# Small columns grouped and padded, so that every wide tile starts on a 512-byte line of its partition

## The chip, the cores and the metric

The kernel runs on one core of one Trainium2 chip. The metric is device time in microseconds (us), the median of three runs; the profile is one execution, taken by the hardware profiler. A core has a matrix engine (PE, whose weight loads are listed as PEld), and DVE, ACT and POOL for elementwise work; SP issues transfers. All tiles here live in the on-chip memory of 128 partitions, and PE writes its results into eight banks of its own (the tiles `pa`, `pb`, `pc`, `pt`).

## What is computed

A two-layer transformer over 512 tokens of 1024 features, in float32. Around each mixer stand two half-weighted gated feed-forward blocks of 2816 hidden features; the first mixer joins sparse and dilated attention, the second is a latent attention.

```python
def _swiglu(x, w_gate, w_up, w_down):
    return (jax.nn.silu(x @ w_gate) * (x @ w_up)) @ w_down
...
def _rms_norm(x, g):
    xf = x.astype(jnp.float32)
    y = xf * lax.rsqrt(jnp.mean(xf * xf, axis=-1, keepdims=True) + NORM_EPS)
    return (y * g.astype(jnp.float32)).astype(x.dtype)
```

The stages run one after another: feed-forward f0, the even mixer (sparse and dilated), f1, f2, the latent mixer, f3, a last norm.

## The kernel before

Features lie on partitions and the 512 tokens along them, so an activation tile is 128 x 512 float32, 2048 bytes of each partition. To keep float32 accuracy every operand is split into a high and a low part, and `mm3` (L142 to L146) makes one product out of three matmuls: weights high with activations high (L144), weights high with activations low (L145), weights low with activations high (L146). Each matmul loads a 128 x 128 block of weights and streams 512 columns of activations past it.

A feed-forward block has two kinds of stretch. Gate and up: for each of 22 hidden tiles, 8 `mm3` into `pa` (gate) and 8 into `pb` (up), with the normalised input `xh`, `xl` as the stream. Down: for each of 8 outputs and each half of the hidden tiles, 11 `mm3` into `pc` or `pt`, with the activations `fah`, `fal` as the stream. The weights come in both cases as chunks of 128 x 1024 (`w`, loaded by SP), split by ACT into `wh` (L128) and by DVE into `wl` (L129); two chunks are held ahead. In the mixers, projections stream `xh`, `xl` too; the even mixer's output projection streams `oh`, `ol`; the latent one's queries and keys stream `cnh`, `cnl`; values are made with the activations as weights and 256 columns of `wh` as the stream.

Where a tile lies on its partition follows from the order in which tiles are first asked for. The pool `keep` lasts for the whole program; `ff`, `ev` and `ml` lie behind it, one after another in the same space. A tile takes its bytes, rounded up to 32. The program starts with 16,512 bytes of other use, 128 bytes past a 512-byte line. So the wide tiles are shifted against the lines by the small ones ahead of them: `x` and `ident` start 128 bytes behind a line; `ones`, `mhalf` and `g` (32 + 32 + 256 bytes) push `xh`, `xl`, `of` and `t` to 448; three `rcol` and two `rv` (160 bytes) push the row factors, `w`, `wh`, `wl` and all that follows to 96; in the even mixer, `pos`, `gt`, `mn` and others push once or twice more. The blocks of 128 columns that one matmul takes of a chunk are 512 bytes wide, so all of them share the chunk's offset.

| tiles (start within a 512-byte line) | before | after |
|---|---|---|
| `xh`, `xl` (stream of gate, up and most projections) | 448 | 0 |
| `w`, `wh`, `wl` (weights of nearly all matmuls) | 96 | 0 |
| `fah`, `fal` (stream of down) | 96 | 0 |
| `oh`, `ol` (stream of the even output projection) | 224 | 0 |
| `cnh`, `cnl` (stream of latent queries and keys) | 96 | 0 |
| `q`, `kh`, `kl`, `v`, `p` of the even mixer | 224 | 0 |
| `ident`, `x` | 128 | 0 |

Of the kernel before, what the change touches and what calls it, by code (L numbers as in the profile page):

```python
# [3 lines left out]
P = 128  # L4
D, SEQ, FF = 1024, 512, 2816
# [8 lines left out]
# column ranges of the even mixer's input projection  # L14
# [3 lines left out]
# blocks of a transposed probability tile: 0 zeros, 1-4 keys 0-127 (queries 0..3), 5-7 keys  # L18
# 128-255 (queries 1..3), 8 keys 384-511 (query 3), 9-10 keys 256-383 (queries 2, 3)
# [10 lines left out]
# The mixers' plans: heads' softmax jobs, and after each the other work. q, k: projections of a pair of  # L30
# heads' queries and keys; v: values; s, c: compression; p: compressed probabilities; o: a chunk of the
# output projection; in the latent mixer l: low-rank inputs, u, w: weights, r: rotary keys.
# [21 lines left out]
def keys(u):  # L54
    """The chunks of weights that a piece of work reads."""
    mla, c, n = u.isupper(), u[0].lower(), u[1:]
    if c == "v" and n in "aA":
        return [("ev_vsw", i) for i in range(3)]
    n = int(n)
    if mla:  # L60
        return {"L": [("mla_in", n)], "W": [("mla_uq", n)], "Y": [("mla_ukv", n)],
                "O": [("mla_out", n)]}.get(u[0], [])
    return {"q": [("ev_in", n)], "k": [("ev_in", n)], "s": [("ev_in", 4 + n)], "o": [("ev_out", n)],
            "c": [("cmp_w1", n, 0), ("cmp_w1", n, 1)], "v": [("ev_vb", n, 0), ("ev_vb", n, 1)]}.get(c, [])


def strided(t, b):
    """Columns 16 n + 2 l + b of t as [partitions, l, n], n < 31."""
    return bass.AP(tensor=t.tensor, offset=t.offset + b, ap=[t.ap[0], [2, 16], [16, 31]])


class Core:
    def __init__(self, tc, ctx, aps):
        self.tc, self.nc, self.a, self.used = tc, tc.nc, aps, -1
        self.keep = ctx.enter_context(tc.tile_pool(name="keep", bufs=1))
        self.ps = ctx.enter_context(tc.tile_pool(name="ps", bufs=2, space=PSUM))
        nc = self.nc
        self.x = [self.keep.tile([P, SEQ], F32, name=f"x{k}") for k in range(KT)]
        self.ident = self.keep.tile([P, P], F32, name="ident")
        self.ones = self.keep.tile([P, 1], F32, name="ones")  # L80
        self.mhalf = self.keep.tile([P, 4], F32, name="mhalf")
        self.g = self.keep.tile([P, 60], F32, name="g")
        nc.vector.memset(self.ones, 1.0)
        nc.vector.memset(self.mhalf, -0.5)
# [15 lines left out]
    def plan(self, stages):  # L100
        """The order in which chunks of weights are used."""
        todo = []
        for st in stages:
            if st in FFNS:
                name, l, _ = FFNS[st]
                for h in range(2):
                    for f in range(h * HF, h * HF + HF):
                        todo += [(name + "_g", l, f), (name + "_u", l, f)]
                    todo += [(name + "_d", l, h, c) for c in range(HF)]
            elif st != "n":  # L110
                for u in flat(EVEN if st == "e" else MLA):
                    todo += keys(u)
        self.todo, self.ready, self.ahead = todo, [], 2

    def fetch(self):
        """Emits the load of the next chunk and, but for compression weights, its split."""
        nc, kp = self.nc, self.keep
        key = self.todo[len(self.ready)]
        src = self.a[key[0]][key[1:]]
        cols = src.shape[1]  # L120
        w = kp.tile([P, 1024], F32, name="w", bufs=3)
        nc.sync.dma_start(w[:, :cols], src)
        if key[0] == "cmp_w1":
            self.ready.append((key, w))
            return
        h = kp.tile([P, 1024], F32R, name="wh", bufs=3)
        l = kp.tile([P, 1024], F32R, name="wl", bufs=3)
        nc.scalar.activation(h[:, :cols], w[:, :cols], AF.Copy)  # L128
        nc.vector.tensor_tensor(l[:, :cols], w[:, :cols], raw(h[:, :cols]), OP.subtract)  # L129
        self.ready.append((key, (h, l)))  # L130

    def chunk(self, *key):
        """A chunk of weights, [128, columns], as its high and low parts; the next ones are under way."""
# [3 lines left out]
        got, tiles = self.ready[i]  # L137
# [10 lines left out]
    def split(self, src, g, tags, bufs):  # L148
        """src [128, 512] times the column g, as high and low parts."""
# [7 lines left out]
    def squares(self, tiles):  # L157
        """Tiles whose features' sum is that of the squares of `tiles`."""
# [10 lines left out]
    def rstd(self, parts, n, before=None):  # L169
        """1/rms over n features from their squares: a column for each block of tokens. With `before`,  # L170
        columns, it is that of the features times `before`, and has this factor in it."""
# [6 lines left out]
        col = kp.tile([P, 4], F32, name="rcol", bufs=3)  # L178
        v = kp.tile([P, 4], F32, name="rv", bufs=2)
# [11 lines left out]
    def spread(self, col, row):  # L191
        """The row `row` of the columns `col`, on all partitions."""
# [58 lines left out]
    def job(self, sb, scores, mask, PT, o, v, start, stop, gate=None, after=None, factor=None):  # L251
        """One head of one branch in three steps: the normalised probabilities [128, (qt, keys)],
        their transposes as high and low parts, and o [(high, low) of V's features, queries] += V . P."""
# [3 lines left out]
        def soft():  # L257
            pt = st["p"] = sb.tile([P, 1280], F32, name="p", bufs=2)
            for qt in range(4):
# [4 lines left out]
                mn = sb.tile([P, 4], F32, name="mn", bufs=8)  # L264
# [34 lines left out]
    @staticmethod  # L299
    def pipe(groups, jobs, do):  # L300
        """Runs a plan, [(names of jobs, other work after each)]: the softmax of a job goes before the
        rest of the job ahead of it."""
# [33 lines left out]
    def values(self, sb, parts, xs, scale=None, more=None):  # L336
        """V of four heads with tokens on partitions: [128, kt, head, (high, low)]. Columns after
        the 256 of V go to `more`."""
# [3 lines left out]
        m = SEQ // c                     # blocks of tokens in a bank  # L342
# [25 lines left out]
    def out_proj(self, oh, parts, name, c):  # L368
        """Chunk c of the output projection, (outputs, pairs of heads, 128): x += its product."""
# [17 lines left out]
    def even(self, gi):  # L387
        nc, a, kp = self.nc, self.a, self.keep
        with self.tc.tile_pool(name="ev", bufs=1, reuse_waits="tile") as sb:
# [16 lines left out]
            nc.gpsimd.tensor_tensor(SR, SR, R, OP.mult)  # L406
            PT = self.pt_tiles(sb)
            q, kd, V, O, C, oh = {}, {}, {}, {}, {}, {}
# [13 lines left out]
            def qstack(i):  # L422
                """Two heads' queries times -1/8, each with its high and low parts stacked."""
# [7 lines left out]
            def kdup(i):  # L431
                """Two heads' keys: high parts twice, low parts twice."""
# [23 lines left out]
            def finish(pair, j):  # L456
                """Fold a head's two parts; after the second head, split the pair."""
# [32 lines left out]
            def stack(i):  # L490
                """Keys or values to compress plus their positions: rows (l mod 2, feature), columns
                (l // 2, group, block)."""
# [14 lines left out]
            def compress(i):  # L507
# [16 lines left out]
                if i == 0:  # L524
                    nc.tensor.matmul(vp[:, :64], w2[:, 0, :], z, start=True, stop=True)
                    kcmp = C["k"] = sb.tile([P, 64], F32, name="kcmp")
                    nc.vector.tensor_copy(kcmp, vp[:, :64])
# [13 lines left out]
            C["g"] = sb.tile([P, 4, 24], F32, name="gt")  # L541

            def gate(kt, p):
                """The sigmoids of a block of tokens' gates."""
# [11 lines left out]
            def cmp_probs(g):  # L556
                """The compressed branch's probabilities for four heads: keys (head, n) on partitions."""
# [7 lines left out]
                st = sb.tile([P, 3, 16], F32, name="st", bufs=2)  # L565
# [38 lines left out]
    def mla(self, gi):  # L604
        nc, a, kp = self.nc, self.a, self.keep
        with self.tc.tile_pool(name="ml", bufs=1, reuse_waits="tile") as sb:
            xs, rc, R = self.norm(gi)
            # even heads have (content, rotary, rotary with its halves swapped) on partitions,
            # odd heads (rotary, swapped, content)
# [18 lines left out]
            def low(i):  # L628
                """The low-rank inputs: queries' but for their tokens' factors (0, 1), keys' and
                values' (2), the keys' rotary part (3)."""  # L630
# [17 lines left out]
            def factors(i):  # L648
                """The tokens' factors: of keys and values (2) or queries (1)."""
# [7 lines left out]
            def rotary(n):  # L657
                """The rotary part of two heads' keys."""
# [94 lines left out]
def constants(np):  # L753
    """Tables that depend on the shapes alone."""
# [3 lines left out]
    d = p + 384 - j                      # query minus key, for the last block of queries  # L758
# [27 lines left out]
def layout(np, i):  # L786
    """The inputs as the chip reads them: each chunk of weights contiguous on its partitions."""
# [14 lines left out]
    def feat(w):  # L802
        """[K, 128 n] -> n chunks [128, (k, 128)]."""
# [3 lines left out]
    def out_parts(w, parts):  # L807
        """[(pair, 128), 1024] -> for each part of the pairs, chunks [128, (outputs, pair, 128)]."""
# [8 lines left out]
    def tok(w, n):  # L817
        """[1024, c] -> chunks [128, (n k, c)]."""
        w = w.reshape(KT, P, -1)
        pad = -KT % n  # L820
        if pad:
# [10 lines left out]
    d["pos"] = np.concatenate([w, w])   # [(group, feature), k or v, l mod 2, l // 2]  # L832
# [8 lines left out]
                 axis=3)                # [k, 128, pair, parity, 128]  # L841
# [24 lines left out]
```

## Time and profile before

| what | value |
|---|---|
| median of 3 runs | 1989.07 us (1989.05 to 1989.41) |
| span of the profiled execution | 1983.8 us |
| time outside the span, against the median | 5.3 us |
| PE busy | 1945.0 us, 98% |
| PEld, DVE, ACT, POOL busy | 81%, 53%, 38%, 21% |
| granted clock of PE, mean | 0.995 |

The page gives the profiled execution by its span, from the first to the last instruction; the time around it is taken from the median. Since PE is busy for 98% of it, the length of one matmul and their number nearly make the time. A matmul's listed duration overlaps with that of the next, so the pace is read from the distance of starts.

### The profile page before, as it was taken

To read this page: it belongs to the slowest core of one execution; us is meant where nothing else is said; L and a number is where in the kernel's file an instruction comes from. 1 tells how busy PE (TensorE), PEld (TensorE's weight loads), DVE (VectorE), ACT (ScalarE), POOL (GpSimd) and SP (SyncE) were. 2 spreads that over 40 slices of the span, in tenths; PEclk is the share of its full clock that TensorE was granted. 3 is DMA by queue.
4 is the path that set the end of the run, shared out by engine and by line. 5 is a ranking of instruction groups with operands and counts; after the bars stand their busy time and mean duration, and the time that the engine had idled before them with its cause. 6 is when DMAs were issued, how large, how long until landed. Compare 5 with 4: busy or idle time off the path is not lost.

```text
span 1983.8 us, 23309 instructions
## 1 busy us (share of the span) xinstructions
PE 1945.0 (98%) x9086; PEld 1601.1 (81%) x9086; DVE 1058.2 (53%) x1594; ACT 754.9 (38%) x1230; POOL 408.2 (21%) x390
## 2 busy tenths in 40 slices
PE   8999999999998999999999999999999999999997
PEld 6888888878887788888888888888878878888885
DVE  5443444467888744344444543554399764434442
ACT  4321223347586532222232222223388543212231
POOL 4110111164445311001110100111156331101111
PEclk9999999999999999999999999999999999999998
DMA  4322222322111132222322232222310223222221
GB/s 161 96 96 95 96 96 96 112 90 96 54 44 33 46 105 95 95 96 96 96 96 95 86 97 99 91 96 96 121 44 22 64 85 96 95 96 96 96 96 54
DMA packets 49422, 174.37 MB, mean 88 GB/s; under 512 B 5792, under 2 KB 6176, under 8 KB 49312
## 3 DMA queue, kind: packets, MB, share of 16 engines
q1 hardware_dynamic: 47808, 169.64, 26.3%
q0 software_dynamic: 640, 2.10, 0.3%
q8 instruction: 71, 1.16, 0.2%
q10 hardware_dynamic: 864, 1.15, 0.2%
q14 instruction: 39, 0.32, 0.1%
HBM read 170.76 MB, written 2.10 MB: 87 GB/s over the span
## 4 chain that ended last, share of the span: by engine, by line
PE 92%; DVE 4%; ACT 2%; POOL 1%; issue 1%; DMA 0%; DVEq 0%; POOLq 0%; ACTq 0%
PE pa L146 11%; PE pa L145 11%; PE pa L144 11%; PE pb L146 9%; PE pb L145 9%; PE pb L144 9%; PE pc L144 4%; PE pc L145 4%; PE pc L146 4%; PE pt L146 4%; PE pt L144 4%; PE pt L145 4%; PE pc L293 2%; PE pt L282 2%; PE pb L452 1%
## 5 line engine op out<-in xcount | busy, mean ns | idle before, releaser
L128 ACT ACTIVATE wh<-w 128x1024 fp32r<-128x1024 f32 (+1 forms) x313 | 331.3, 1059 | 894.5 <-issue 347.3
L129 DVE TENSOR_TENSOR wl<-w,wh 128x1024 fp32r<-128x1024 f32 (+1 forms) x313 | 482.1, 1541 | 234.9 <-ACT wh L128 234.7
L144 PE MATMUL pa<-xh,wh 128*128 128x512 f32 x928 | 368.2, 397 | 8.6 <-ACT xh L153 8.1
L146 PE MATMUL pa<-xh,wl 128*128 128x512 f32 x928 | 369.1, 398 | 0.0
L145 PE MATMUL pa<-xl,wh 128*128 128x512 f32 x928 | 367.7, 396 | 0.3 <-DVE xl L154 0.3
L232 POOL TENSOR_TENSOR fa<-fs,fu 128x512 f32<-128x512 f32 x88 | 117.9, 1339 | 1070.3 <-DVE fu L228 636.9
L146 PE MATMUL pb<-xh,wl 128*128 128x512 f32 x704 | 280.0, 398 | 0.0
L145 PE MATMUL pb<-xl,wh 128*128 128x512 f32 x704 | 278.5, 396 | 0.1
L144 PE MATMUL pb<-xh,wh 128*128 128x512 f32 x704 | 277.5, 394 | 0.0
L144 PEld LDWEIGHTS pa<-xh,wh 128*128 128x128 f32 x928 | 174.9, 188 | 50.0 <-ACT xh L153 8.1
L228 DVE TENSOR_TENSOR fu<-pb,rrow 128x512 f32<-128x512 f32 x88 | 60.8, 691 | 280.8 <-PE pb L146 280.8
L145 PEld LDWEIGHTS pa<-xl,wh 128*128 128x128 f32 x928 | 174.8, 188 | 43.4 <-DVE xl L154 1.6
L146 PEld LDWEIGHTS pa<-xh,wl 128*128 128x128 f32 x928 | 174.8, 188 | 40.5 <-DVE wl L129 0.2
L145 PEld LDWEIGHTS pb<-xl,wh 128*128 128x128 f32 x704 | 132.3, 188 | 35.8 <-DVE xl L154 2.5
L144 PEld LDWEIGHTS pb<-xh,wh 128*128 128x128 f32 x704 | 132.4, 188 | 32.2 <-ACT xh L153 0.4
L146 PEld LDWEIGHTS pb<-xh,wl 128*128 128x128 f32 x704 | 132.2, 188 | 30.8 <-DVE wl L129 0.2
L226 DVE TENSOR_TENSOR fg<-pa,rrow 128x512 f32<-128x512 f32 x88 | 60.8, 691 | 147.5 <-PE pa L146 147.4
L145 PE MATMUL pc<-fal,wh 128*128 128x512 f32 x352 | 137.1, 389 | 0.0
L144 PE MATMUL pc<-fah,wh 128*128 128x512 f32 x352 | 137.0, 389 | 0.0
L146 PE MATMUL pc<-fah,wl 128*128 128x512 f32 x352 | 136.9, 389 | 0.0
L146 PE MATMUL pt<-fah,wl 128*128 128x512 f32 x352 | 136.9, 389 | 0.0
L144 PE MATMUL pt<-fah,wh 128*128 128x512 f32 x352 | 136.9, 389 | 0.0
(184 smaller groups left out, 2737.4 us busy)
## 6 DMA issues: line engine op xcount, KB each, us to landing
w<-f_g SPq DMA_DIRECT2D x88, 512.0 KB, 3.4
w<-f_u SPq DMA_DIRECT2D x88, 512.0 KB, 3.4
w<-f_d SPq DMA_DIRECT2D x88, 512.0 KB, 3.4
w<-ev_in SPq DMA_DIRECT2D x16, 512.0 KB, 3.4
w<-ev_out SPq DMA_DIRECT2D x8, 512.0 KB, 3.6
w<-mla_out SPq DMA_DIRECT2D x8, 512.0 KB, 3.6
x<-x POOLq DMA_DIRECT2D x8, 256.0 KB, 7.0
w<-ev_vb SPq DMA_DIRECT2D x4, 512.0 KB, 3.6
```

Of the source, the lines that this page charges most:

```text
L128: nc.scalar.activation(h[:, :cols], w[:, :cols], AF.Copy)
L129: nc.vector.tensor_tensor(l[:, :cols], w[:, :cols], raw(h[:, :cols]), OP.subtract)
L144: nc.tensor.matmul(out, wh, xh, start=start, stop=False)
L145: nc.tensor.matmul(out, wh, xl, start=False, stop=False)
L146: nc.tensor.matmul(out, wl, xh, start=False, stop=stop)
L226: nc.vector.tensor_tensor(t, pgu[0], R, OP.mult)
L228: nc.vector.tensor_tensor(u, pgu[1], R, OP.mult)
L232: nc.gpsimd.tensor_tensor(a, s, u, OP.mult)
L282: nc.tensor.transpose(ps[:, i * P:(i + 1) * P], pt[:, c:c + P], self.ident)
L293: nc.tensor.matmul(ps[:, q0:], v(kt), PT[j][:, b, :], start=start and kt == 0 and j == 0, stop=stop and kt == 3 and j == 1)
L452: nc.tensor.matmul(ps[:, :n], q[qi][:, qt * P:(qt + 1) * P], kd[ki][j][:, :n], start=j == 0, stop=j == 1)
```

## The change

No operation is added, dropped or moved: on each engine the instructions stand in the same order, with the same shapes, and the transfers too. Three small columns and `rv` are asked for ahead of everything, `rcol` gets 16 buffers instead of 3 (16 x 32 = 512 bytes), the small tiles of the even mixer are asked for together ahead of the wide ones (the two `st` as tiles of their own instead of two buffers), and `mn` has 16 buffers instead of 8 in the latent mixer. With that each group of small tiles fills whole lines together with what stands around it, and every wide tile starts at 0. As by-products, some reuses of a column buffer are gone, and with them a second semaphore of one POOL, four ACT and ten DVE instructions that wait for another one anyway. Comments and document strings are dropped as well, so line numbers after differ.

```diff
+        self.small()
         self.x = [self.keep.tile([P, SEQ], F32, name=f"x{k}") for k in range(KT)]
         self.ident = self.keep.tile([P, P], F32, name="ident")
...
+    def small(self):
+
         self.ones = self.keep.tile([P, 1], F32, name="ones")
         self.mhalf = self.keep.tile([P, 4], F32, name="mhalf")
         self.g = self.keep.tile([P, 60], F32, name="g")
...
+        self.rv()
+
+    def rv(self):
+        return self.keep.tile([P, 4], F32, name="rv", bufs=2)
...
-        col = kp.tile([P, 4], F32, name="rcol", bufs=3)
-        v = kp.tile([P, 4], F32, name="rv", bufs=2)
+        col = kp.tile([P, 4], F32, name="rcol", bufs=16)
+        v = self.rv()
...
-                mn = sb.tile([P, 4], F32, name="mn", bufs=8)
+                mn = self.stats(sb)
...
+    def stats(sb):
+
+        return sb.tile([P, 4], F32, name="mn", bufs=8 if sb.name == "ev" else 16)
...
+            q, kd, V, O, C, oh = {}, {}, {}, {}, {}, {}
+            C["g"] = sb.tile([P, 4, 24], F32, name="gt")
+            C["k"] = sb.tile([P, 64], F32, name="kcmp")
+            C["st"] = [sb.tile([P, 3, 16], F32, name=f"st{g}") for g in range(2)]
+            self.stats(sb)
             PT = self.pt_tiles(sb)
-            q, kd, V, O, C, oh = {}, {}, {}, {}, {}, {}
...
-                st = sb.tile([P, 3, 16], F32, name="st", bufs=2)
+                st = C["st"][g]
```

## Rows read from the trace of the kernel before

**Rows 1.** The page: span; busy time of the engines; granted clock of PE by slice.

```profile
span 1983.8 us, 23309 instructions
...
PE 1945.0 (98%) x9086; PEld 1601.1 (81%) x9086; DVE 1058.2 (53%) x1594; ACT 754.9 (38%) x1230; POOL 408.2 (21%) x390
...
PEclk9999999999999999999999999999999999999998
```

**Rows 2.** The chain that ended last, shares of the span by engine.

```profile
PE 92%; DVE 4%; ACT 2%; POOL 1%; issue 1%; DMA 0%; DVEq 0%; POOLq 0%; ACTq 0%
```

**Rows 3.** Windows: stretch, length, busy us of PE, PEld, DVE, ACT, POOL, clock, DMA.

```profile
60.00:130.00 70.00, 70.00 (x301) 56.31 (x300) 35.20 (x32) 20.29 (x25) 8.03 (x7) 1.00 0.29 92
150.00:184.00 34.00, 34.00 (x152) 28.16 (x151) 10.63 (x11) 6.37 (x6) 0.00 (x0) 1.00 0.31 99
720.00:790.00 70.00, 70.00 (x302) 56.31 (x301) 33.44 (x31) 19.66 (x24) 7.75 (x6) 1.00 0.30 98
820.00:854.00 34.00, 34.00 (x152) 28.15 (x151) 10.48 (x11) 6.37 (x6) 0.00 (x0) 1.00 0.29 93
```

**Rows 4.** Timeline of PE in gate and up of f0: start, duration, instruction.

```profile
100.60 0.39 PE L144 MATMUL pb<-xh,wh 128*128 128x512 f32 x1
100.83 0.39 PE L145 MATMUL pb<-xl,wh 128*128 128x512 f32 x1
101.07 0.40 PE L146 MATMUL pb<-xh,wl 128*128 128x512 f32 x1
101.30 0.39 PE L144 MATMUL pb<-xh,wh 128*128 128x512 f32 x1
```

**Rows 5.** Timeline of PE in down of f0, a triple's start and the next one's.

```profile
160.14 0.39 PE L144 MATMUL pt<-fah,wh 128*128 128x512 f32 x1
...
160.82 0.39 PE L144 MATMUL pt<-fah,wh 128*128 128x512 f32 x1
```

**Rows 6.** Groups of instructions by line: count, then busy us and mean ns.

```profile
L144 PE MATMUL pa<-xh,wh 128*128 128x512 f32 x928 | 368.2, 397 | 8.6 <-ACT xh L153 8.1 <-DVE x L384 0.5
...
L144 PE MATMUL pb<-xh,wh 128*128 128x512 f32 x704 | 277.5, 394 | 0.0
...
L144 PE MATMUL pc<-fah,wh 128*128 128x512 f32 x352 | 137.0, 389 | 0.0
...
L144 PE MATMUL pt<-fah,wh 128*128 128x512 f32 x352 | 136.9, 389 | 0.0
...
L144 PE MATMUL pa<-oh,wh 128*128 128x512 f32 x64 | 25.9, 412 | 4.8 <-DVE x L384 4.7
```

**Rows 7.** Timeline of PE, even output projection, five triples apart.

```profile
665.52 0.39 PE L144 MATMUL pa<-oh,wh 128*128 128x512 f32 x1
...
669.01 0.39 PE L144 MATMUL pa<-oh,wh 128*128 128x512 f32 x1
```

**Rows 8.** Timeline of PE, a latent query's six matmuls and what follows.

```profile
1456.93 0.40 PE L144 MATMUL pa<-cnh,wh 128*128 128x512 f32 x1
...
1458.32 0.27 PE L282 MATMUL pt<-ident,p 128*128 128x128 f32 x1
```

**Rows 9.** Timeline of PE, values of the even mixer, four triples apart.

```profile
381.26 0.28 PE L351 MATMUL pa<-wh,xh 128*128 128x256 f32 x1
...
382.67 0.28 PE L351 MATMUL pa<-wh,xh 128*128 128x256 f32 x1
```

**Rows 10.** Timeline of PE, values of the latent mixer, two triples apart.

```profile
1440.71 0.28 PE L351 MATMUL pa<-wh,cnh 128*128 128x256 f32 x1
...
1441.43 0.28 PE L351 MATMUL pa<-wh,cnh 128*128 128x256 f32 x1
```

**Rows 11.** Waits: who waited for whom, us in total, times, longest.

```profile
POOL rcol L186 <- DVE rv L181: 58.4, 7, 12.5
...
ACT p L268 <- DVE mn L265: 29.7, 31, 2.7
...
PE pa L144 <- ACT xh L153: 8.1, 1, 8.1
```

More of the change, by code (lines that the diff above doesn't have):

```diff
@@ L77, in __init__ @@
         nc = self.nc
+        self.small()
         self.x = [self.keep.tile([P, SEQ], F32, name=f"x{k}") for k in range(KT)]
         self.ident = self.keep.tile([P, P], F32, name="ident")
+        nc.vector.memset(self.ones, 1.0)
+        nc.vector.memset(self.mhalf, -0.5)
+    def small(self):
         self.ones = self.keep.tile([P, 1], F32, name="ones")
@@ L82, in __init__ @@
         self.g = self.keep.tile([P, 60], F32, name="g")
-        nc.vector.memset(self.ones, 1.0)
-        nc.vector.memset(self.mhalf, -0.5)
+        self.rv()
+    def rv(self):
+        return self.keep.tile([P, 4], F32, name="rv", bufs=2)
     def load(self):
@@ L297, in job @@
         return soft, trans, pv
+    @staticmethod
+    def stats(sb):
+        return sb.tile([P, 4], F32, name="mn", bufs=8 if sb.name == "ev" else 16)
     @staticmethod
@@ L525, in compress @@
                     nc.tensor.matmul(vp[:, :64], w2[:, 0, :], z, start=True, stop=True)
-                    kcmp = C["k"] = sb.tile([P, 64], F32, name="kcmp")
-                    nc.vector.tensor_copy(kcmp, vp[:, :64])
+                    nc.vector.tensor_copy(C["k"], vp[:, :64])
                     return
@@ L539, in compress @@
                         nc.vector.tensor_tensor(vc[s, j, 64:128], vg[s], raw(vc[s, j, 0:64]), OP.subtract)
-            C["g"] = sb.tile([P, 4, 24], F32, name="gt")
             def gate(kt, p):
```

## Prediction

> **What bounds the kernel now.** First the page: PE is busy for 1945.0 of 1983.8 us, with its clock granted in full nearly throughout, that is at 2.4 GHz [rows 1]. Then the chain of work that ended last: 92% of it is PE [rows 2], and PE's longest wait in the whole program, 8.1 us, is the start-up [rows 11]. So a change reaches the time by the pace of matmuls, or not at all; what DVE, ACT, POOL and the transfers do counts only where PE waits for them, and that is under 39 us (1983.8 - 1945.0), spread over start, end and the mixers.
>
> Next the pace, stage by stage, in the windows [rows 3]. Two stretches of gate and up, 70 us each, hold 300 matmuls (301 and 302 with those cut at the edges): 70.0 / 300 = 233.3 ns each. Two stretches of down, 34 us each, hold 150: 226.7 ns. In both PE is busy throughout and the granted clock is 1.00. The timeline shows the same without an average: one `mm3` takes 0.70 us in gate and up (100.60 to 101.30) [rows 4] and 0.68 us in down (160.14 to 160.82) [rows 5].
>
> This is the row on which all rests. The two kinds of stretch issue the same thing, weight blocks of 128 columns and streams of 512 in the order of L144 to L146, yet one is 3% slower. Four things differ: where the stream lies (448 against 96 bytes behind a line, weights at 96 in both), the result banks, the length of a group (24 against 33 matmuls), and what the other engines do meanwhile. The last can be struck out: DVE is busy for half of gate and up (35.20 of 70) and ACT for under a third (20.29) [rows 3], in pieces, while the triple stays at 0.70 us whether or not they run. What is left is the place of the stream, or the banks and group length.
>
> A third place helps. In the even output projection, with the stream at 224 and weights at 96, five triples take 669.01 - 665.52 = 3.49 us, 232.7 ns a matmul [rows 7], into the bank that gate uses. So three distances between stream and weights give three paces: 0 bytes 226.7, 128 bytes 232.7, 352 bytes 233.3 ns. Equal offsets give the shortest.
>
> **The change, part by part.** (1) Gate and up. After the change stream and weights both start at 0, so their distance is 0 as in down today. Of triples into `pb` there are 704, all from the blocks; into `pa` 928, of which 704 are gate and 224 projections [rows 6]. So 1408 triples go from 0.70 to 0.68 us: 1408 x 0.020 = 28.2 us saved. The stretch must then not meet another bound. Down already runs at 0.68 us a triple with the same chunks to split, at DVE 10.63 and ACT 6.37 of 34 us [rows 3], and gate and up leave half of DVE free; they are 3% shorter afterwards, no more.
>
> (2) The mixers' wide matmuls: 224 triples with `xh`, `xl` and 64 with `oh`, `ol` [rows 6]. There PE hops between short groups. A query of the latent mixer has equal offsets already (96 and 96), and its six matmuls take 1458.32 - 1456.93 = 1.39 us, 231.7 ns each [rows 8], not 226.7. So equal offsets bring 233.3 - 231.7 = 1.6 ns at least and 6.6 ns at most: 672 x 1.6 = 1.1 us to 672 x 6.6 = 4.4 us for the projections, and 192 x (232.7 - 231.7) = 0.2 us to 192 x 6.0 = 1.2 us for the output projection. These groups are nearest to the query's, so I take 2.0 us of the 1.3 to 5.6.
>
> (3) Shorter streams. Values of the even mixer, with unlike offsets, need (382.67 - 381.26) / 12 = 117.5 ns for 256 columns [rows 9]; those of the latent mixer, with equal ones, (1441.43 - 1440.71) / 6 = 120 ns [rows 10]. Equal offsets do not help there and might cost 2.5 ns on 288 matmuls of this kind, 0.7 us; I take 0.3. Transposes and single columns show no unlike pair to compare; I take 0.
>
> (4) Down stays at 0 distance: 0 in the likeliest case; its bounds are in the rivals.
>
> (5) The other engines' operations and the transfers read and write from new places. What hides them is PE: without that cover only the 8.1 us of the start and the few waits in the mixers show it, and a few per cent of these is under 1 us. I take 0.
>
> (6) The dropped second semaphores: POOL's reciprocal roots waited 58.4 us for DVE [rows 11], and the softmax exponentials 29.7 us for DVE, so the other semaphore was never last. 0.
>
> Sum: 28.2 + 2.0 - 0.3 = 29.9 us. The profiled span becomes 1983.8 - 29.9 = 1953.9; with 5.3 us around it (1989.07 - 1983.8) that is 1959.2 us.
>
> A rule of the Trainium skill speaks against this. Its page "TensorE: Matmul & The Clock Gate", section "Step-by-step: what each phase is for", gives PE two independent read ports, so that loading the next weights takes nothing from the running matmul; by that the place of one against the other would not matter and the sum would be 0. The trace does not fit it well: the page's gap of about 216 ns for 512 columns is 226.7 at best here, and the gap does differ between stretches.
>
> **The rivals.** *No change.* The 3% come from the banks or the group length, and offsets do nothing. For it: `pa` and `pb` hold the triples of 0.70 us and `pc` and `pt` those of 0.68, without exception in the long stretches. Against it: the bank `pa` shows 231.7 with equal offsets [rows 8] and 232.7 and 233.3 with unlike ones; that is little, since the first comes from short groups. Time: 1989. The Trainium skill's page "SBUF — State Buffer", section "Specifications (TRN2)", gives on-chip lines of 16 bytes; by that rule, too, nothing would move, as 96, 224 and 448 are all multiples of 16. The rows here show no such line.
>
> *The place behind the line counts, not the distance.* 96, 224 and 448 bytes behind a line give 226.7, 232.7 and 233.3: the pace also falls with the offset itself. Then 0 is better than 96, and down gains as well. A straight line through the first two gives 222.2 ns at 0, one through the outer two 224.9. Gate and up would save 1408 x 3 x 11.1 = 46.9 or x 8.4 = 35.5 us, down 704 x 3 x 4.5 = 9.5 or x 1.8 = 3.8 us, with the 2 us of the mixers 58.4 or 41.3 in all: 1931 to 1948. Against it: three points, and the step from 224 to 448 is small.
>
> *Slower.* A start on a multiple of 64 bytes costs: 448 is one and pays 233.3, 96 is not and pays 226.7. After the change all starts are such multiples; gate and up keep 0.70 us and down goes from 0.68 to 0.70: 704 triples (352 into each of two banks [rows 6]) x 0.020 = 14.1 us, 2003 us. It decides as soon as gate and up gain less than 14.1 us, that is when their triple stays above 0.69. Against it: 224 is no such multiple and pays 232.7.
>
> **How the numbers follow.** Equal distance, as forecast: 0.57, with a range of its own of 1955 to 1961 (the bounds of parts 2 and 3). The place behind the line: 0.14. No change: 0.17. Slower: 0.08. What I have not thought of: 0.04, half of it slower and a quarter each faster and the same. The runs before lie within 0.36 us, and under 0.2%, 4 us, I call it no change. So faster 0.57 + 0.14 + 0.01 = 0.72, the same 0.17 + 0.01 = 0.18, slower 0.08 + 0.02 = 0.10. The range reaches from the upper end of the second case, 1945 (a fifth of it kept), over the forecast to no change, 1990: 0.57 + 0.03 + 0.17 + 0.02 = 0.79. It leaves out most of the second case and the slower one.
>
> **What would show it.** In gate and up, a triple of 0.68 us, 309 matmuls in 70 us; in down 0.68 as before. If gate and up reach 0.68 and down falls below, the place behind the line counts. If both stand as they were, it was banks or groups. If down rises to 0.70, it is the multiple of 64. Groups of the other engines should keep their mean durations where no other engine disturbs them, and PE's waits should stay at some 39 us. I am wrong if the pace depends on the pair in a way that three distances do not show, for instance if 0 and 0 collide where 96 and 96 do not, or if the faster PE runs ahead of the split of a chunk, which would appear as waits of PE for `wh` or `wl`.

## The result: 1957.5 us after 1989.1, and the profile after

The changed kernel takes 1957.49 us (median of four runs, 1954.03 to 1958.47) against 1989.06 (1988.98 to 1989.41) for the kernel before: a ratio of 0.9838 with an interval of 0.9824 to 0.9852. The profiled execution took 1958.47 us with a span of 1956.7.

The page after, to be read beside [rows 1] and [rows 2]:

```profile
span 1956.7 us, 23295 instructions
...
PE 1916.9 (98%) x9086; PEld 1604.4 (82%) x9086; DVE 1057.6 (54%) x1594; ACT 754.9 (39%) x1230; POOL 407.7 (21%) x390
...
PE 93%; DVE 4%; ACT 2%; issue 1%; POOL 0%; DMA 0%; DVEq 0%; ACTq 0%; POOLq 0%
```

As many matmuls as before (9086), and 28.1 us less of PE busy; DVE, ACT and POOL within 0.6 us of where they were. So PE's pace changed, and the busy times of the others did not. The windows of the kernel after say where; columns as in [rows 3], gate and up in the first and third, down in the second and fourth:

```profile
60.00:128.00 68.00, 68.00 (x301) 56.33 (x301) 34.31 (x32) 19.94 (x26) 7.75 (x6) 1.00 0.31 97
150.00:184.00 34.00, 34.00 (x151) 28.16 (x151) 10.64 (x11) 6.99 (x7) 0.00 (x0) 1.00 0.29 93
720.00:788.00 68.00, 68.00 (x302) 56.31 (x301) 34.35 (x32) 19.93 (x26) 7.75 (x6) 1.00 0.31 97
820.00:854.00 34.00, 34.00 (x152) 28.15 (x151) 10.67 (x11) 7.23 (x7) 0.00 (x0) 1.00 0.31 100
```

Gate and up now issue in 68 us the 301 matmuls that took 70 [rows 3]; down issues what it did. The granted clock is 1.00 in both kernels here, so it isn't the clock. Without an average, from the timeline of PE after (start, duration, instruction): 48 triples apart in gate and up, then 32 apart in down.

```profile
61.19 0.39 PE L152 MATMUL pa<-xh,wh 128*128 128x512 f32 x1
...
93.83 0.39 PE L152 MATMUL pa<-xh,wh 128*128 128x512 f32 x1
...
151.63 0.39 PE L152 MATMUL pc<-fah,wh 128*128 128x512 f32 x1
...
173.39 0.39 PE L152 MATMUL pt<-fah,wh 128*128 128x512 f32 x1
```

(93.83 - 61.19) / 48 = 0.680 us a triple, and (173.39 - 151.63) / 32 = 0.680. A matmul is still shown as 0.39 us long, as in [rows 4]: its duration overlaps the next one's, and only the distance between starts shows the pace.

The whole span can be laid out by one kind of instruction, the sums of the norms, which open and close the stages. From the chain of work that ended last (start, us, what; seven of these rows in each kernel), before:

```profile
24.33 1.68 PE pt L176 x16
384.01 1.46 PE pt L176 x14
688.07 1.68 PE pt L176 x16
1051.79 1.46 PE pt L176 x14
1419.25 1.46 PE pt L176 x14
...
1610.22 1.68 PE pt L176 x16
1968.68 1.74 PE pt L176 x14
```

and after:

```profile
24.40 1.68 PE pt L184 x16
377.45 1.46 PE pt L184 x14
682.59 1.68 PE pt L184 x16
1039.43 1.46 PE pt L184 x14
1399.87 1.46 PE pt L184 x14
...
1589.36 1.68 PE pt L184 x16
1941.11 2.36 PE pt L184 x14
```

Differences of neighbouring rows are the stages. The four feed-forward blocks become shorter by 6.63 (359.68 to 353.05), 6.88, 7.02 and 6.71 us, 27.24 together; the latent mixer becomes shorter by 1.48; the even mixer becomes longer by 1.08 (304.06 to 305.14), the end by 0.47 and the start by 0.07. Sum: 27.1 us saved, the difference of the spans.

The even mixer is longer although a quiet stretch of its output projection is quicker (shown with the mixers below). Windows of PE alone in it (length, busy us and matmuls, granted clock, DMA share, GB/s), before:

```profile
425.00:440.00 15.00, 12.03 (x62) 0.89 0.33 102
500.00:512.00 12.00, 9.39 (x54) 1.00 0.17 47
```

and after:

```profile
425.00:440.00 15.00, 12.08 (x58) 0.77 0.40 128
500.00:512.00 12.00, 8.94 (x42) 0.86 0.15 44
```

The two pairs don't hold quite the same work, since the mixer begins 6.6 us earlier after the change. In both stretches PE had waited (12 of 15 and some 9 of 12 us busy). The granted clock was at its lower level, 1.2 GHz, for a part of the first stretch before (0.89), and for a part of both after (0.77 and 0.86). Such stretches also differ between runs of one kernel: the runs after have mean clocks of 0.993 to 0.996 and spans of 1956.7 to 1952.3 us, and later runs of the kernel before go from 1985.88 us at 0.995 to 1990.45 at 0.992. The profiled execution of the kernel before was a short one: time and span lie some 1.8 us apart in every run here that lists both, so a span of 1983.8 stands for some 1985.6 us, 3.5 below the median.

### The profile page after: what moved, and what is told of

Its sections match the earlier page's. It is cut to its first block, busy times and chain, and to the rows that moved or that the text cites. A ratio compares the mean times of both kernels' runs of the same rounds, so it can differ in the third digit from the quotient of the medians.

```text
span 1956.7 us, 23295 instructions
## 1 busy us (share of the span) xinstructions
PE 1916.9 (98%) x9086; PEld 1604.4 (82%) x9086; DVE 1057.6 (54%) x1594; ACT 754.9 (39%) x1230; POOL 407.7 (21%) x390
## 4 chain that ended last, share of the span: by engine, by line
PE 93%; DVE 4%; ACT 2%; issue 1%; POOL 0%; DMA 0%; DVEq 0%; ACTq 0%; POOLq 0%
PE pa L152 11%; PE pa L153 11%; PE pa L154 11%; PE pb L153 9%; PE pb L154 9%; PE pb L152 9%; PE pt L154 4%; PE pc L154 4%; PE pc L152 4%; PE pt L152 4%; PE pc L153 4%; PE pt L153 4%; PE pc L301 2%; PE pt L290 2%; PE pb L469 1%; DVE wl L137 1%
## 5 line engine op out<-in xcount | busy, mean ns | idle before, releaser
L136 ACT ACTIVATE wh<-w 128x1024 fp32r<-128x1024 f32 (+1 forms) x313 | 331.3, 1059 | 867.0 <-issue 352.1
L137 DVE TENSOR_TENSOR wl<-w,wh 128x1024 fp32r<-128x1024 f32 (+1 forms) x313 | 481.8, 1540 | 235.5 <-ACT wh L136 234.9
L153 PE MATMUL pa<-xl,wh 128*128 128x512 f32 x928 | 363.3, 391 | 0.0
L154 PE MATMUL pa<-xh,wl 128*128 128x512 f32 x928 | 362.9, 391 | 0.0
L240 POOL TENSOR_TENSOR fa<-fs,fu 128x512 f32<-128x512 f32 x88 | 117.5, 1335 | 1043.8 <-DVE fu L236 974.3
L154 PE MATMUL pb<-xh,wl 128*128 128x512 f32 x704 | 274.3, 390 | 0.0
L153 PE MATMUL pt<-fal,wh 128*128 128x512 f32 x352 | 136.9, 389 | 0.0
```

The costliest lines, as they stand in the source:

```text
L153: nc.tensor.matmul(out, wh, xl, start=False, stop=False)
L154: nc.tensor.matmul(out, wl, xh, start=False, stop=stop)
L240: nc.gpsimd.tensor_tensor(a, s, u, OP.mult)
```

## The experiments

**Theory and rivals.** The theory is that the pace depends on where the stream lies against the weights. The rivals are the stream's own place behind a line, a start on a line, a start on a multiple of 64 bytes, and the banks or the length of a group.

**1. Equal distance, off the line.** The kernel before with 352 unused bytes, which move weights and the stream of down from 96 to 448, where the stream of gate and up already lies.

```diff
     # in rms, ahead of rrow
+    self.pad = getattr(self, "pad", None) or self.keep.tile([P, 88], F32, name="pad")
```

> The kernel before with one unused tile of 352 bytes ahead of the row factors: weights and down's stream move from 96 to 448, the place where the stream of gate and up already lies; nothing starts on a line. Equal distance (forecast): gate and up 0.68 us a triple, down 0.68, time 1989.1 - 28.2 - about 1 = 1960 us; the even output projection keeps 128 bytes of distance (64 against 448) and stays near 232 ns a matmul. Place of the stream (448 is a bad place whatever the weights do): gate and up stay at 0.70 and down rises to 0.70, 1989.1 + 14.1 = 2003 us. Start on a line needed: not below 1989 us.

1960.96 us (1959.11 to 1961.22), ratio 0.9856 (0.9842 to 0.9871). Windows as above, gate and up, then down:

```profile
60.00:128.00 68.00, 68.00 (x302) 56.31 (x301) 34.34 (x32) 19.93 (x26) 7.75 (x6) 1.00 0.28 99
150.00:184.00 34.00, 34.00 (x152) 28.15 (x151) 10.61 (x11) 7.03 (x7) 0.00 (x0) 1.00 0.26 93
```

The pace is that of the changed kernel with both at 448, a multiple of 64 and not on a line. The stream of gate and up hasn't moved at all. So three rivals fall: its own place, the start on a line, and the multiple of 64.

**2. On the line, but apart.** The changed kernel with 160 unused bytes: the stream of gate and up stays at 0, weights and the stream of down go to 160.

```diff
     # in rms, ahead of rrow
+    self.pad = getattr(self, "pad", None) or self.keep.tile([P, 40], F32, name="pad")
```

> The changed kernel with 160 unused bytes ahead of the row factors: the stream of gate and up stays at 0, weights and down's stream go to 160, so gate and up have again the distance of before (352 = -160 in 512), and down has equal offsets off the line. Equal distance: gate and up 0.70 us, down 0.68, time 1957.5 + 28.2 + about 1 = 1987 us. Start of the stream on a line suffices: gate and up 0.68, time about 1958 us.

1987.81 us (1985.03 to 1989.11, ten runs), ratio 0.9993 (0.9983 to 1.0003), as before.

```profile
60.00:128.00 68.00, 68.00 (x293) 54.72 (x292) 34.04 (x31) 20.19 (x25) 8.02 (x7) 1.00 0.27 93
150.00:184.00 34.00, 34.00 (x152) 28.15 (x151) 10.63 (x11) 6.37 (x6) 0.00 (x0) 1.00 0.29 100
```

Gate and up are back at 293 matmuls in 68 us, 0.70 us a triple; down, whose stream moved along with its weights, is untouched. Banks and groups are those of the changed kernel. Distance alone gives the whole gain back.

**3 and 4. A map of distances.** The feed-forward blocks alone (both mixers left out); the eight tiles of x lie at 0, 64, ..., 448 bytes, so that every group runs through eight places; then the same with weights moved by 192 bytes (the last line of the edit).

```diff
-        h = self.keep.tile([P, SEQ], F32R, name=tags + "h", bufs=bufs)
+        self.nsplit = getattr(self, "nsplit", -1) + 1
+        c = (0, 16, 32, 48, 64, 80, 96, 112)[self.nsplit % 8]
+        h = self.keep.tile([P, SEQ + 128], F32R, name=tags + "h", bufs=bufs)[:, c:c + SEQ]
...
+    self.pad = getattr(self, "pad", None) or self.keep.tile([P, 48], F32, name="pad")
```

> Feed-forward blocks and last norm alone (both mixers left out), weights at 0, and the eight tiles of the normalised input at 0, 64, 128, ... 448 bytes, one place for each k. Equal distance: k = 0 at 226.7 ns a matmul, k = 2 (128 bytes) near 232.7, the others slower than 226.7; the mean of a group of 24 between 226.7 and 233.3. Multiples of 64 alone: all eight alike. Down at 0 and 0: 0.68 us a triple.

> As the map of 64 steps, with the weights at 192 instead of 0 (mixers left out). Equal distance: the same eight paces, moved by three places: k = 3 at 226.7 ns, k = 5 (128 bytes) as k = 2 of the first map. Place of the stream: the same eight paces at the same k as in the first map.

One run each: 1496.48 and 1495.90 us. Timeline of PE in the first kernel, four tiles of one group (0, 64, 128 and 192 bytes) and the next start:

```profile
102.16 0.39 PE L152 MATMUL pa<-xh,wh 128*128 128x512 f32 x1
...
102.85 0.40 PE L152 MATMUL pa<-xh,wh 128*128 128x512 f32 x1
...
103.55 0.40 PE L152 MATMUL pa<-xh,wh 128*128 128x512 f32 x1
...
104.25 0.39 PE L152 MATMUL pa<-xh,wh 128*128 128x512 f32 x1
...
104.94 0.39 PE L152 MATMUL pa<-xh,wh 128*128 128x512 f32 x1
```

0.69, 0.70, 0.70, 0.69: neighbours of unlike places blur each other, and the order of 64, 128 and 192 bytes here isn't that of the single distances below. What can be read off is the period, in the medians over all groups. For 0, 64, ..., 448 bytes they are 690, 698, 697, 695, 690, 698, 697, 695 ns: the row repeats after 256 bytes, not after 512. With weights at 192: 698, 697, 695, 690, 698, 697, 695, 690. The same row moved by three places of 64: it follows the distance, and the distance counts modulo 256.

**5 to 7. One distance for a whole block**, which takes the blur out: the same edit with one place for each of the four blocks (still without mixers).

```diff
-        c = (0, 16, 32, 48, 64, 80, 96, 112)[self.nsplit % 8]
+        c = (4, 8, 16, 32)[self.nsplit // 8]     # then (1, 2, 24, 40), then (48, 56, 60, 64)
```

> Feed-forward blocks and last norm alone (both mixers left out), weights at 0; the stream of gate and up lies at one place for a whole block, 16 bytes behind the weights' place in f0, 32 in f1, 64 in f2, 128 in f3. Step (any distance that is no multiple of 256 costs the same): 0.70 us a triple in all four. Smooth growth with distance: 16 and 32 near 0.68, 64 and 128 near 0.70. Down, at 0 and 0, 0.68 in all.

> As the kernel with 16, 32, 64 and 128 bytes (mixers left out), with distances 4, 8, 96 and 160. Step: 0.70 in all four. A whole line or word of 16 or more bytes counts, not the byte: 4 and 8 as 0, 0.68, and 96 and 160 0.70. 96 must repeat the kernel before (352 = 256 + 96), 0.70.

> As the kernel with 16, 32, 64 and 128 bytes (mixers left out), with distances 192, 224, 240 and 256. Period of 256 bytes: 256 at 0.68 us a triple. Period of 512: 256 at 0.70. Only the size of the distance to the next multiple of 256 counts: 192, 224 and 240 as 64, 32 and 16.

1496.82, 1507.50 and 1495.87 us. From pairs of starts 48 triples apart, as above, a triple takes, in us:

```
bytes   4     8     16    32    64    96    128   160   192   224   240   256
        0.710 0.700 0.695 0.700 0.687 0.700 0.697 0.703 0.700 0.700 0.700 0.680
```

From the timeline of PE, each in its own kernel: 4 bytes, the slowest, then 64, then 256.

```profile
61.40 0.40 PE L152 MATMUL pa<-xh,wh 128*128 128x512 f32 x1
...
95.47 0.40 PE L152 MATMUL pa<-xh,wh 128*128 128x512 f32 x1
```

```profile
821.55 0.39 PE L152 MATMUL pb<-xh,wh 128*128 128x512 f32 x1
...
854.51 0.39 PE L152 MATMUL pb<-xh,wh 128*128 128x512 f32 x1
```

```profile
1161.24 0.39 PE L152 MATMUL pb<-xh,wh 128*128 128x512 f32 x1
...
1193.88 0.39 PE L152 MATMUL pb<-xh,wh 128*128 128x512 f32 x1
```

256 bytes is as good as 0; every other distance tried costs 7 to 30 ns a triple, without a smooth course; none goes below 0.68. Nor do the two sides mirror each other: 192 and 240 bytes cost 0.700, 64 and 16 bytes 0.687 and 0.695. The kernel before fits in: 448 against 96 is 352, which is 96 modulo 256 and costs 0.700 here as there; its output projection, 128 apart, showed 0.698 [rows 7].

One distance has two paces. The table reads the first half of each block's gate and up, and the second half agrees with it but for 128 bytes, where a triple takes (1383.92 - 1350.32) / 48 = 0.700 us instead of 0.697:

```profile
1350.32 0.40 PE L152 MATMUL pa<-xh,wh 128*128 128x512 f32 x1
...
1383.92 0.40 PE L152 MATMUL pa<-xh,wh 128*128 128x512 f32 x1
```

So at an unlike place something else can shift the pace by 3 ns a triple; no run here says what.

**8 and 9. The cheapest version, beside the change once more.** The kernel before with 96 unused bytes: weights at 192, 256 bytes from the stream of gate and up; nothing on a line, and the even output projection still 128 apart.

```diff
     # in rms, ahead of rrow
+    self.pad = getattr(self, "pad", None) or self.keep.tile([P, 24], F32, name="pad")
```

> The kernel before with one unused tile of 96 bytes: weights and down's stream move from 96 to 192, the stream of gate and up stays at 448, so its distance becomes 256; nothing starts on a line. Period of 256 bytes: gate and up 0.68 us a triple, down 0.68, 1989 - 28 - about 1 = 1960 us. Same place within a 512-byte line needed: gate and up 0.70, 1989 us.

> The changed kernel once more, on the same chip as the pad of 96 bytes: about 1957.5 us. What it gains over the pad of 96 bytes is what the even mixer's equal offsets bring, 0 to 2 us, if the runs are close enough to tell.

1958.70 us (1957.23 to 1961.05), ratio 0.9849 (0.9833 to 0.9866), against 1957.97 (1955.69 to 1958.48), 0.9842 (0.9827 to 0.9857), for the changed kernel measured along with it. Windows of the former:

```profile
60.00:128.00 68.00, 68.00 (x301) 56.31 (x300) 34.49 (x32) 19.98 (x25) 7.75 (x6) 1.00 0.28 98
150.00:184.00 34.00, 34.00 (x151) 28.15 (x150) 10.45 (x11) 7.18 (x7) 0.00 (x0) 1.00 0.26 93
```

One tile that nobody uses brings what the regrouping and padding of all tiles brings; the 0.7 us between them lie inside the spread of either. No version here beats the changed kernel.

**10. One of three weight blocks apart.** The changed kernel's feed-forward blocks (no mixers), everything at 0 but `wl` at 96.

```diff
-        l = kp.tile([P, 1024], F32R, name="wl", bufs=3)
+        l = kp.tile([P, 1152], F32R, name="wl", bufs=3)[:, 24:1048]
```

> Feed-forward blocks and last norm alone (both mixers left out), all at 0 but the low weights, which lie at 96. The stream meets the load of the next weights: the low weights are loaded while L153's stream runs, so the step from L153 to L154 grows from 226.7 to about 233, the other two stay, and a triple takes about 0.687 us, in gate and up and in down. The stream meets its own weights: the step from L154 to the next L152 grows instead. Any unlike pair slows all: 0.70 us.

1511.68 us. Windows, gate and up, then down:

```profile
60.00:128.00 68.00, 68.00 (x294) 54.90 (x293) 34.22 (x31) 20.29 (x25) 7.78 (x7) 1.00 0.30 93
150.00:184.00 34.00, 34.00 (x148) 27.44 (x147) 10.62 (x11) 6.37 (x6) 0.00 (x0) 1.00 0.30 94
```

A triple takes 0.698 us in both. All three steps of a triple lengthen, to medians of 232 to 233 ns, though two of them use `wh`, which lies as before. So this run doesn't tell which load meets which stream. It does show down slowed by a distance, in its own banks and with its own length of group.

## Why the prediction was right, step by step

**Gate and up (part 1).** Right: 0.70 to 0.68 us a triple, as forecast. The blocks gave 27.2 us of the 28.2; the rest may be the beginnings and ends of stages, where the steady pace doesn't hold, but no run measured that. Down kept its 0.68 (part 4), and the splits by ACT and DVE kept their durations (part 5): 331.3 and 481.8 us for their 313 instructions each after, 331.3 and 482.1 before. They did not become PE's bound. The prediction's sign of being wrong, a wait of PE for `wh`, shows once, in the latent mixer, and costs nothing: 0.8 us there wait for ACT's `wh` after, and 0.8 us waited for DVE's `t` before.

**The mixers (parts 2 and 3).** A saving of 2.0 us was forecast, less 0.3 for the values; the profiled spans show 0.4 (1.48 - 1.08). But they don't compare like with like. The even mixer as a whole, PE alone, columns as above: before, in experiment 2's kernel, and after.

```profile
384.01:688.07 304.06, 292.58 (x1678) 0.99 0.19 62
```

```profile
383.99:690.79 306.80, 295.95 (x1680) 0.98 0.18 61
```

```profile
377.45:682.59 305.14, 292.45 (x1679) 0.98 0.19 62
```

Experiment 2's kernel is no quicker than the kernel before in gate and up, and it has the longest even mixer, at a lower clock than before. So the lower clock doesn't come from the quicker PE; the kernel before was profiled in an execution with little of it. Against experiment 2's kernel, whose `xh` and `xl` are again apart from their weights while the streams of its even output projection are not, the change saves 1.66 us in the even mixer and 1.19 in the latent one, 2.85 together. What the clock can do to a stage is seen in the latent mixer of experiment 1 and of the changed kernel, where the wide streams lie at their weights' place in both:

```profile
1400.69:1591.31 190.62, 185.27 (x1010) 0.98 0.15 51
```

```profile
1399.87:1589.36 189.49, 184.06 (x1009) 0.99 0.17 51
```

They differ by 1.13 us. So the two comparisons give 0.4 and 2.9 us, the clock can move either by about as much, and the net 1.7 of the forecast is neither confirmed nor refuted. The size of this term stays open.

The pace moved the way it was forecast in places: five triples of the even output projection in its quiet stretch now take (663.04 - 659.64) / 15 = 226.7 ns a matmul, where [rows 7] gave 232.7.

```profile
659.64 0.39 PE L152 MATMUL pa<-oh,wh 128*128 128x512 f32 x1
...
663.04 0.39 PE L152 MATMUL pa<-oh,wh 128*128 128x512 f32 x1
```

In the time that projection's own share was not measurable: the kernel with 96 bytes, which leaves it unlike, is 0.7 us away. The values of 256 columns became slower, as bounded: 18 of them take 376.08 - 373.93 = 2.15 us, 119.4 ns, for 117.5 in [rows 9]. So equal offsets are not good for every shape.

**The sum and what lies around it.** 29.9 us were forecast; the profiled spans give 27.1 and the medians 31.6. From the profiled execution of experiment 2 to that of the change, with mean clocks of 0.992 and 0.993, it is 29.4 (1986.1 - 1956.7), though experiment 2's even output projection already has stream and weights at one place. One step was misread, at no cost to the forecast: the 5.3 us "around" the span were 1.8 us and a short execution. Taken with the right 1.8 us and a median 3.5 us above the profiled run, the forecast sum gives the same time. For the same reason the 0.36 us between three runs was too narrow a measure of the spread: later runs of the kernel before lie up to 4.6 us apart.

**The rivals.** *No change, by banks or groups*: `pa` and `pb` now show 0.68, experiment 2 slows gate and up in the same banks, and experiment 10 slows down in its own. The Trainium skill's "TensorE: Matmul & The Clock Gate", section "Step-by-step: what each phase is for", whose two independent read ports, as the prediction read them, would make the sum 0, does not fit: a triple takes 0.680 to 0.710 us as the relative address is changed. *The place behind the line*: down would have fallen below 0.68 and did not, and experiment 1 has the gain at 448. *Slower on multiples of 64*: all starts are such multiples after the change, and 0.68 holds. The 16-byte lines of the Trainium skill's "SBUF — State Buffer", section "Specifications (TRN2)", do not account for it either: 16, 32 and 64 bytes are all multiples and cost 0.695, 0.700 and 0.687.

**What is shown and what is not.** It is shown that these matmuls are quickest, 0.680 us a triple, where stream and weights are a multiple of 256 bytes apart, and slower at each other distance tried, and that this is the whole of what the change gained in gate and up. It is not shown what inside the chip makes an unlike pair slower, which load meets which stream, why 128 bytes has two paces, or how much the mixers gained.

## What to carry to other kernels

Where PE runs float32 matmuls of 512 columns back to back with a weight load for each, as here, put stream and weights at the same place modulo 256 bytes of a partition; one unused tile can be enough, so look at the offsets before rebuilding a layout. For streams of 256 columns the runs show no gain. The sign in a profile is two stretches of the same instructions, both without waits and at the full clock, with unlike distances between starts while the durations look alike. Judge a gain under 4 us here by several runs, since stretches at the lower clock move a single one by that much.

## What was unexpected

The period is 256 bytes, not the 512 of the change. The cost has no smooth course: 64 bytes apart costs 7 ns a triple, 4 bytes 30. Moving only one of the three weight blocks of a triple slows all three steps, by some 6 ns each. And the even mixer came out longer after a change that quickens PE. That goes with the clock of single executions, not with the change: experiment 2's kernel, as slow as before in gate and up, spent longer still there.
